# The order of eight heads in a decoder layer's attention: four differential, then four sparse

## The chip, the cores and the metric

The kernel runs on one core of a Trainium2 chip. The metric is the device time of one execution in microseconds (us); the median of several runs is compared.

## What is computed

One decoder layer over 528 tokens (512 and 16 meta tokens) of width 1024: half of a SwiGLU FFN, an attention with two groups of heads side by side, an output projection, and half of a second FFN. The reference, cut to the attention (its two functions compute the queries in blocks of 128):

```python
# differential group, 4 heads, two score maps each (m = 0, 1)
s = einsum('bqhmd,bkhmd->bhmqk', q, k) * A_SCALE + bias
p = softmax(where(k_pos <= q_pos, s, -inf))
a = p[:, :, 0] - lam * p[:, :, 1]
o_a = rmsnorm(einsum('bhqk,bkhd->bqhd', a, v), subln_g) * (1 - lam_init)

# sparse group, 4 heads, one score map each, over the 128 keys
# that an indexer's scores select for every query
_, sel = top_k(score, topk)
s = einsum('bqhc,bqkc->bhqk', q_lat, c[sel]) * B_SCALE + bias
o_b = einsum('bqhc,hcd->bqhd', einsum('bhqk,bqkc->bqhc', softmax(s), c[sel]), w_uv)

h = h + concat([o_a, o_b]) @ w_out
```

All values are 32-bit floats.

## The kernel before

Everything is one program written with a library that records instructions and orders them engine by engine. A matrix product is split into three, of a high and a low part of each operand (hi by hi, hi by lo, lo by hi), so that each product appears as three matmuls. High parts are made by ScalarE (ACT), low parts by VectorE (DVE), as a difference.

The attention works through a list `units` (line 907): for each head in a written-out order, its four blocks of 128 queries (t = 0 to 3, with 144, 272, 400 and 528 keys). `n` is 32 units. A pair (0, hd) in the list is a differential head, (1, hd) a sparse one. The list is the line that the change touches:

```python
    for kind, hd in ((0, 0), (0, 1), (0, 2), (1, 0), (0, 3), (1, 1), (1, 2), (1, 3)):
        units += [(kind, hd, t) for t in range(NQ)]
```

A loop over `i` (from line 1211) pipelines the units. In one pass, unit i has its scores reduced and exponentiated (`u_soft`, lines 999 and 1005), unit i - 1 is normalized (`u_norm`), unit i - 2 is transposed and split (`u_trans`, `u_high`, `u_low`), and the scores of unit i + 1 are computed (`u_scores`).

- `u_scores`: a differential unit has two maps with 64 rows of contraction (line 980), a sparse one a single map with two times 128 rows (line 986). Both are six matmuls per unit, twelve for the 528 keys, which take two pieces of 264. The results go to three PSUM banks, tag "s", used in turn.
- `u_soft`: DVE adds the bias and takes the minimum on the way out of PSUM (line 999, one instruction and a tiny read per map and piece), ACT exponentiates (line 1005).
- `u_norm`: DVE scales and subtracts two maps for a differential unit (lines 1017, 1018), scales one for a sparse unit (line 1020).
- `u_trans`, `u_high`, `u_low`: TensorE (PE) transposes the weights (lines 1027, 1029), ACT makes the high parts, DVE the low parts (lines 1044, 1045). The fourth block is followed by a small cast on DVE (line 1231).
- `u_mask`: for a sparse unit GpSimd (POOL) adds the bias and the selection mask into one of two buffers (line 965).

When a head's fourth block is split, a chain of small steps is started for it and advanced twice per pass. `head_a` multiplies by the values (13 matmuls, line 1054) and normalizes (lines 1064 to 1095). `head_b` multiplies by the latent values twice (26 matmuls), then by `w_uv` (line 1111).

Two more kinds of work lie in the same passes. The latent queries of the sparse heads, `q_latent(hd)`, are made in four chains: 12 matmuls (line 1126), a root mean square, a scaling on DVE (line 1139, four instructions), eight transposes on PE (line 1144) and their splits (lines 1146, 1147). The chain of head hd is started by

```python
        for hd in range(A_H):
            if i == max(QS + 2 * hd, units.index((0, hd, NQ - 1))):
                qchains.append(q_latent(hd))
```

with QS = 7, that is at i = 7, 9, 11 and 19, since the chain of head 3 waits for the fourth block of differential head 3. And once the differential heads 0 to 2 are finished, the output projection is begun for these three heads ahead of time, one eighth (`wo_step`, lines 1162 to 1180) at most of the passes.

The selection of the 128 keys is made by DVE in 16 rounds per block (`topk_round`, lines 759 and 760, and line 763 at the end). These rounds are recorded with a lower priority, so that the library puts them between other work; the last ones, of the fourth block, stand among the units of the fourth head in the list. The bias of the next head is fetched by a DMA on POOL's queue when the scores of the third block are computed (`load_bias`).

Of the kernel before, what the change touches and what calls it, by code (L numbers as in the profile page):

```python
# [200 lines left out]
def layer(ctx: ExitStack, tc: tile.TileContext, xT, gcols, kvg, lamv, rel, onehot,  # L201
# [703 lines left out]

    uku, uvu, buf = [], [], {}
    units = []
    for kind, hd in ((0, 0), (0, 1), (0, 2), (1, 0), (0, 3), (1, 1), (1, 2), (1, 3)):
        units += [(kind, hd, t) for t in range(NQ)]
    n = len(units)  # L910
    st = {}
# [299 lines left out]
    while i < n or chains or qchains or st:  # L1211
# [16 lines left out]
        if 0 <= i - 2 < n and units[i - 2][2] == NQ - 1:  # L1228
            kind, hd, t = units[i - 2]
# [134 lines left out]
```

## Time and profile before

| | |
|---|---|
| median of 3 runs | 1070.76 us (1066.65 to 1071.95) |
| the profiled execution | 1067.94 us, span 1066.2 us |
| PE busy | 1039.1 us, 97% of the span |
| DVE busy | 756.2 us, 71% |
| ACT busy | 522.4 us, 49% |
| mean granted TensorE clock | 0.986 |
| the attention's units | about 483 to 690 us |

The span is the time from the first to the last instruction. The granted clock is TensorE's clock as a share of its full speed: 1.00 is 2.4 GHz, 0.50 is 1.2 GHz. In rows with several engines, "busy (x)" is the time in which the engine had an instruction, and their number. Matmuls overlap their neighbours, so that a matmul's own duration is longer than the step from one start to the next.

### The profile page before, as it was taken

What the parts mean: (1) busy time and instruction counts of PE and PEld (TensorE: products, weight loads), DVE (VectorE), ACT (ScalarE), POOL (GpSimd) and SP (SyncE); (2) the same over time, 40 slices, a digit from 0 to 9 for tenths busy, and PEclk for the clock granted to TensorE, in tenths of its full rate; (3) what the DMA queues carried; (4) which work ended last, traced back from release to release, by engine and by line L of the source; (5) the groups of instructions that cost most, each with busy time, mean ns of one, the idle gap of its engine ahead of it and who ended that gap; (6) DMA issues with size and microseconds to landing.
All of it is one profiled execution on the core that took longest, in us unless ns stands there. A gap on an engine that the chain in (4) does not pass through costs nothing.

```text
span 1066.2 us, 18282 instructions
## 1 busy us (share of the span) xinstructions
PE 1039.1 (97%) x7185; PEld 955.2 (90%) x7185; DVE 756.2 (71%) x1485; ACT 522.4 (49%) x1057; POOL 49.5 (5%) x57
## 2 busy tenths in 40 slices
PE   7999999999999999998999899999999999999998
PEld 7999999999999997997887688788889999988886
DVE  7968999985232246898999878667979999852231
ACT  6626666654222254564546565355546666631111
POOL 0000000000010110000000111030000000000000
PEclk9999999999999999998999789999999999999999
DMA  6263323234333332120220015453333333343331
GB/s 241 80 223 110 101 98 118 87 122 129 104 114 99 116 106 84 60 71 21 90 70 29 20 29 160 144 185 101 117 121 118 103 100 119 129 136 105 116 114 35
DMA packets 38403, 112.58 MB, mean 106 GB/s; under 512 B 4866, under 2 KB 6146, under 8 KB 38316
## 3 DMA queue, kind: packets, MB, share of 16 engines
q1 hardware_dynamic: 36236, 105.64, 30.6%
q0 software_dynamic: 1792, 5.48, 1.5%
q8 instruction: 56, 0.92, 0.3%
q10 hardware_dynamic: 288, 0.29, 0.1%
q14 instruction: 31, 0.25, 0.1%
HBM read 102.98 MB, written 11.44 MB: 107 GB/s over the span
## 4 chain that ended last, share of the span: by engine, by line
PE 87%; DVE 8%; ACT 2%; issue 1%; DMA 1%; ACTq 0%; DVEq 0%
PE d L432 24%; PE X L193 16%; PE V L193 8%; PE g L432 6%; PE u L432 5%; PE nat L708 4%; PE Y L193 4%; PE wo L1162 3%; PE p_ch L925 2%; PE p_ch L664 2%; PE p_ch L1054 2%; PE iq L664 2%; PE p_ch L1162 2%; PE p_s L980 1%; PE p_s L986 1%
## 5 line engine op out<-in xcount | busy, mean ns | idle before, releaser
L101 DVE TENSOR_TENSOR wl<-wr,wh 128x1024 fp32r<-128x1024 f32 (+4 forms) x106 | 120.8, 1142 | 158.8 <-ACT wh L100 157.7
L100 ACT ACTIVATE wh<-wr 128x1024 fp32r<-128x1024 f32 (+4 forms) x106 | 105.4, 995 | 249.1 <-PE d L432 149.2
L432 PE MATMUL d<-AR,wh 128*128 128x264 f32 (+1 forms) x928 | 184.6, 311 | 0.0
L432 PEld LDWEIGHTS d<-AR,wh 128*128 128x128 f32 x928 | 139.5, 188 | 9.8
L193 PE MATMUL X<-AR,ws 128*128 128x256 f32 (+1 forms) x912 | 117.5, 280 | 0.2
L432 PE MATMUL d<-AR,wl 128*128 128x264 f32 (+1 forms) x464 | 115.5, 310 | 0.0
L193 PEld LDWEIGHTS X<-AR,ws 128*128 128x128 f32 x912 | 111.0, 188 | 1.0 <-ACT FA L498 0.8
L174 ACT ACTIVATE ws<-h 128x512 fp32r<-128x512 f32 x140 | 87.7, 628 | 45.4 <-PE X L193 20.4
L175 DVE TENSOR_TENSOR ws<-h,ws 128x512 fp32r<-128x512 f32 x140 | 95.9, 687 | 13.4 <-ACT ws L174 12.2
L432 PEld LDWEIGHTS d<-AR,wl 128*128 128x128 f32 x464 | 75.6, 188 | 4.9
L708 PE MATMUL nat<-wh,hg 128*128 128x256 f32 (+1 forms) x304 | 57.6, 284 | 0.0
L708 PEld LDWEIGHTS nat<-wh,hg 128*128 128x128 f32 x304 | 47.8, 188 | 0.1
L925 PE MATMUL p_ch<-wh,hg 128*128 128x256 f32 x224 | 44.1, 295 | 0.3 <-DVE AR L878 0.3
L708 PE MATMUL nat<-wl,hg 128*128 128x256 f32 (+1 forms) x152 | 43.1, 283 | 0.0
L193 PE MATMUL X<-hg,ws 128*128 128x264 f32 x312 | 42.4, 285 | 0.0
L193 PE MATMUL V<-hg,ws 128*128 128x264 f32 x312 | 42.3, 285 | 0.0
L582 DVE SCALAR_TENSOR_TENSOR h<-d,h 128x528 f32<-128x528 f32 (+1 forms) x16 | 11.2, 700 | 41.1 <-PE d L432 41.1
L432 PE MATMUL d<-hg,wh 128*128 128x512 f32 x128 | 40.0, 393 | 0.0
L193 PEld LDWEIGHTS X<-hg,ws 128*128 128x128 f32 x312 | 39.9, 188 | 0.0
L193 PEld LDWEIGHTS V<-hg,ws 128*128 128x128 f32 x312 | 39.8, 188 | 0.0
L193 PE MATMUL V<-AR,ws 128*128 128x256 f32 x312 | 39.6, 276 | 0.0
L1005 ACT ACTIVATE FA<-FA,mn 128x144 f32<-128x144 f32 (+3 forms) x48 | 27.3, 570 | 25.0 <-DVE mn L999 24.8
(311 smaller groups left out, 2277.9 us busy)
## 6 DMA issues: line engine op xcount, KB each, us to landing
wr<-w1u SPq DMA_DIRECT2D x17, 512.0 KB, 3.6
wr<-w2u SPq DMA_DIRECT2D x17, 512.0 KB, 3.5
wr<-w1d SPq DMA_DIRECT2D x16, 512.0 KB, 3.4
wr<-w2d SPq DMA_DIRECT2D x16, 512.0 KB, 3.5
wr<-w2g SPq DMA_DIRECT2D x15, 512.0 KB, 3.5
wr<-w1g SPq DMA_DIRECT2D x14, 512.0 KB, 3.5
wr<-win_n SPq DMA_DIRECT2D x12, 512.0 KB, 3.4
wr<-win_t SPq DMA_DIRECT2D x9, 512.0 KB, 3.4
```

The source lines that it names most:

```text
L100: self.nc.scalar.activation(hi[:, c], r[:, c], AF.Copy)
L101: (low or self.low).tensor_sub(lo[:, c], r[:, c], f32(hi[:, c]))
L174: self.nc.scalar.activation(hi, x, AF.Copy)
L175: V.tensor_sub(lo, x, f32(hi))
L193: self.nc.tensor.matmul(ps, l[:, w], self.rhs(q, r, k), start=(p in FIRST and k == 0 and x == 0), stop=(k == KC // 2 - 1 and x == 2), skip ...
L432: PE.matmul(ps[:, i, : b - a], w[:, k, :], x(kk)[:, a:b], start=(kk == 0 and p_ == 0), stop=(kk == ktot - 1 and p_ == 2))
L664: PE.matmul(o, w[:, k, :], x[:, k, a:b], start=(k == 0 and p_ == 0), stop=(k == KC - 1 and p_ == 2))
L708: PE.matmul(ps, xx[:, kk, a:b], w[:, k, :], start=(kk == 0 and p_ == 0), stop=(kk == KC - 1 and p_ == 2))
L925: PE.matmul(ps, xx[:, kk, a:b], w[:, kk % 4, :], start=(kk == 0 and p_ == 0), stop=(kk == KC - 1 and p_ == 2))
L1005: A.activation(s, s, AF.Exp, scale=-1.0, bias=mn, accum_out=sums[:, m: m + 1])
L1054: PE.matmul(oo, l, r, start=(x == 0), stop=(x == len(seq) - 1))
L1162: PE.matmul(ps, w[:, k, :], x[k0 + k], start=(k == 0 and p_ == 0), stop=(k == nk - 1 and p_ == 2))
```

## The change

The list of heads is written in another order. Nothing else is edited.

```diff
-    for kind, hd in ((0, 0), (0, 1), (0, 2), (1, 0), (0, 3), (1, 1), (1, 2), (1, 3)):
+    for kind, hd in ((0, 0), (0, 1), (0, 2), (0, 3), (1, 0), (1, 1), (1, 2), (1, 3)):
         units += [(kind, hd, t) for t in range(NQ)]
```

The head at place p uses buffer `bsel[p]` for its weights and bias table p % 2, so differential head 3 and sparse head 0 change buffers with their places. The chain `q_latent(3)` now starts at i = 15. `q_latent(0)` to `q_latent(2)` and the passes of the output projection stay where they were.

The instructions are the same; what moves is their order. On PE, before, from the last scores of sparse head 0 to the transposes of the latent query of head 2 (p_s are the score banks, p_tr and p_ch other banks, FA holds scores and weights, buf_ql the latent query):

```order
L986 MATMUL p_s<-AR 128x264 x5
L1069 MATMUL p_ch<-onesr,buf_vv 128x1 x4
L980 MATMUL p_s<-AR 128x144 x3
L1027 MATMUL p_ch<-ident,FA 128x128 x2
L1029 MATMUL p_ch<-ident,FA 16x128
L1144 MATMUL p_ch<-ident,buf_ql 128x128 x4
L1027 MATMUL p_tr<-ident,FA 128x128 x3
L1029 MATMUL p_tr<-ident,FA 16x128
L980 MATMUL p_s<-AR 128x144 x3
```

The same place with the change, between the chain of differential head 2 and the transposes of the latent query of head 2:

```order
L1069 MATMUL p_ch<-onesr,buf_vv 128x1 x4
L980 MATMUL p_s<-AR 128x264 x3
L1027 MATMUL p_ch<-ident,FA 128x128 x2
L1029 MATMUL p_ch<-ident,FA 16x128
L980 MATMUL p_s<-AR 128x264 x6
L1027 MATMUL p_tr<-ident,FA 128x128 x3
L1029 MATMUL p_tr<-ident,FA 16x128
L986 MATMUL p_s<-AR 128x144 x6
L986 MATMUL p_s<-AR 128x272 x6
L986 MATMUL p_s<-AR 128x400 x4
L1078 MATMUL p_ch<-ident,ray 4x128
L1144 MATMUL p_ch<-ident,buf_ql 128x128 x4
```

The scores of differential head 3 (line 980) have come ahead, and 16 score matmuls of sparse head 0 (line 986) stand in one piece ahead of the transposes of line 1144.

On DVE, before, from the last round of the selection to the scaling of that latent query (line 1139):

```order
L760 MATCH_REPLACE FA<-m_5415,FA 128x528
L307 SCALAR_TENSOR_TENSOR rqw<-rqw,rqy 128x4
L1045 TENSOR_TENSOR hg<-p_tr,hg 16x128
L763 TENSOR_SCALAR FA<-FA 128x528
L308 SCALAR_TENSOR_TENSOR rqy<-rqw,rqy 128x4
L1014 RECIPROCAL rs<-sums 128x1
L1095 TENSOR_TENSOR AR<-R,AR 128x512
L1139 TENSOR_SCALAR buf_ql<-buf_ql,rqy 128x256 x4
```

With the change, from the same round on:

```order
L760 MATCH_REPLACE FA<-m_5415,FA 128x528
L999 ISA FA,mn<-p_s,FA 128x400
L999 ISA mn 128x1
L763 TENSOR_SCALAR FA<-FA 128x528
L1044 TENSOR_TENSOR hg<-p_tr,hg 128x128
L1045 TENSOR_TENSOR hg<-p_tr,hg 16x128
L1014 RECIPROCAL rs<-sums 128x2
L1095 TENSOR_TENSOR AR<-R,AR 128x512
L1017 TENSOR_SCALAR FA<-FA,rs,lam 128x400
L999 ISA FA,mn<-p_s,FA 128x264
L999 ISA mn 128x1
L1018 SCALAR_TENSOR_TENSOR FA<-FA,rs 128x400
```

The scaling of line 1139 now follows 13 rows after the last of these, behind the other reductions of differential head 3's fourth block; the reduction of 400 keys and the first one of 264 keys are those that free the two banks which the last scores of that block need.

## Rows read from the trace of the kernel before

**Rows 1.** The page: PE's busy time, and the granted clock in 40 slices.
```profile
PE 1039.1 (97%) x7185; PEld 955.2 (90%) x7185; DVE 756.2 (71%) x1485; ACT 522.4 (49%) x1057; POOL 49.5 (5%) x57
...
PEclk9999999999999999998999789999999999999999
```

**Rows 2.** Windows: stretch, its length, busy time of each engine, clock, DMA share, GB/s.
```profile
580.00:600.00 20.00, 17.30 (x117) 13.95 (x113) 18.87 (x65) 14.83 (x49) 2.40 (x3) 1.00 0.05 14
600.00:620.00 20.00, 18.11 (x62) 12.96 (x63) 13.89 (x44) 8.94 (x27) 3.15 (x4) 0.50 0.05 15
```

**Rows 3.** Windows of the attention (PE, PEld, DVE, ACT, POOL, then the clock).
```profile
486.00:488.00 2.00, 0.07 (x1) 0.07 (x1) 1.97 (x8) 0.03 (x1) 0.00 (x0) 0.88 0.00 0
...
598.00:600.00 2.00, 0.18 (x2) 0.00 (x0) 1.94 (x7) 0.53 (x2) 0.34 (x1) 1.00 0.00 0
600.00:602.00 2.00, 0.39 (x2) 0.32 (x2) 2.00 (x5) 0.00 (x0) 1.70 (x2) 0.54 0.00 0
...
618.00:620.00 2.00, 2.00 (x8) 1.81 (x8) 0.69 (x1) 1.54 (x5) 0.00 (x0) 0.50 0.00 0
620.00:622.00 2.00, 2.00 (x12) 1.84 (x11) 0.62 (x2) 1.50 (x5) 0.00 (x0) 0.84 0.00 0
...
601.60:620.60 19.00, 18.71 (x64) 13.56 (x65) 12.29 (x42) 9.54 (x29) 1.75 (x3) 0.50 0.05 16
586.30:602.30 16.00, 11.97 (x77) 10.11 (x77) 14.99 (x45) 9.45 (x35) 3.79 (x3) 0.93 0.06 17
```

**Rows 4.** What PE waited for, 440 to 690 us (total, times, longest).
```profile
PE p_ch L1144 <- DVE buf_ql L1139: 3.4, 1, 3.4
PE p_s L980 <- DVE mn L999: 3.0, 1, 3.0
```

**Rows 5.** Order of time on PE (start, length, line, shape, count, idle before).
```profile
592.99 1.78 PE L1054 MATMUL p_ch<-h,AR 128*128 128x512 f32 x11
...
601.61 1.27 PE L1144 MATMUL p_ch<-ident,buf_ql 128*128 128x128 f32 x4 [3.42 <-DVE buf_ql L1139]
...
618.43 5.25 PE L1054 MATMUL p_ch<-hg,AR 128*128 128x512 f32 x25
623.62 0.87 PE L980 MATMUL p_s<-AR 64*128 64x264 f32 x8
...
638.20 0.28 PE L1126 MATMUL p_ch<-wh,AR 128*128 128x256 f32 x1
638.32 0.28 PE L1126 MATMUL p_ch<-wl,AR 128*128 128x256 f32 x1
...
659.17 1.63 PE L986 MATMUL p_s<-AR 128*128 128x264 f32 x12
```

**Rows 6.** Order of time on DVE, 586 to 628 us.
```profile
586.18 0.16 DVE L308 SCALAR_TENSOR_TENSOR ray<-raw,ray 128x4 f32<-128x4 f32 x1
...
600.16 2.18 DVE L1139 TENSOR_SCALAR buf_ql<-buf_ql,rqy 128x256 f32<-128x256 f32 x4
...
604.37 0.41 DVE L1044 TENSOR_TENSOR hg<-p_ch,hg 128x256 fp32r<-128x256 f32 x1
...
612.10 0.42 DVE L1231 CAST hg<-hg 16x512 fp32r<-16x512 f32 x1
...
627.80 1.14 DVE L1139 TENSOR_SCALAR buf_ql<-buf_ql,rqy 128x256 f32<-128x256 f32 x4
```

**Rows 7.** DVE's busy time, one line each: 999 (two stretches), 1017, 1018, 1020.
```profile
587.50:605.30 17.80, 2.24 (x10) 0.86 0.05 16
605.40:626.80 21.40, 4.32 (x20) 0.64 0.04 10
...
609.00:624.60 15.60, 1.25 (x3) 0.63 0.05 13
...
609.00:624.60 15.60, 1.50 (x3) 0.63 0.05 13
...
587.50:605.30 17.80, 1.05 (x3) 0.86 0.05 16
```

## The prediction

> **What bounds the kernel now.** I read the page first, then the kernel in stretches of 20 us, then the attention in stretches of 2 us, then what TensorE (PE) waited for there, and last the order of time on PE and VectorE (DVE). The page says that PE is busy for 97% of the span and that the chain of work is PE's [rows 1]; a stretch in which PE stands still, or runs at half clock, is therefore paid in full. The profile's clock line has three slices below 9 (8, 7 and 8), all in the attention [rows 1]. By 20 us, DVE is the fuller engine up to 600 us (18.87 of 20 us, PE 17.30), and from 600 to 620 us PE runs at a granted 0.50, 1.2 instead of 2.4 GHz [rows 2].
>
> The reader is to see three things in the finer views. First, PE stood still before both falls of the clock: 3.0 us for DVE's score reduction and 3.4 us for DVE's scaling of the latent query of head 2 [rows 4]. In the first case the clock's mean in 486 to 488 is 0.88, so it fell while PE did next to nothing (0.07 us) [rows 3]; in the second PE was busy for 0.18 and 0.39 us of two 2 us stretches, and the clock went from 1.00 to 0.54 in the second of them [rows 3]. Second, the half clock stayed although PE was then busy almost without a break: 18.71 of 19.00 us [rows 3]. It rose in the stretch 620 to 622, after PE had gone over to the 25 value matmuls that start at 618.43 [rows 3, 5]. At half clock half of the busy time is lost, 18.7 / 2 = 9.4 us. Third, DVE sets the pace before the fall: from 586.3 to 602.3 it is busy 14.99 of 16.00 us [rows 3].
>
> **What the change moves.** No instruction is added or removed. Differential head 3 goes from the fifth place to the fourth, sparse head 0 from the fourth to the fifth. The order is the same up to the square-root refinement that DVE ends at 586.34 (start 586.18, 0.16 long) [rows 6], and again from the scores of sparse head 3 on; all terms lie between. A differential unit costs DVE more: head 3's ten score reductions take 4.32 us, head 0's five 2.24; normalizing its first three blocks takes 1.25 + 1.50 us, where three blocks of the sparse head take 1.05 [rows 7].
>
> *DVE up to the latent query of head 2.* Before, 16.0 us, to 602.34 [rows 6]. Now all of head 3's reductions stand in this piece, 4.32 us, where three of head 0's five stood (2.24 less 0.42, 0.49 and 0.05: 1.3 us); and its normalizing, 2.75 us, where two blocks of the sparse head stood (two thirds of 1.05: 0.7 us). One more split of weights comes in (0.41) [rows 6], and three tiny instructions beside it, for which I take as much again. That is 3.0 + 2.05 + 0.8 = 5.9 us more. Two things go: the scaling took 2.18 us while GpSimd was busy for 1.70 of 2 us, and 1.14 elsewhere [rows 3, 6], and those additions of GpSimd come later now (1.0 us); and DVE's own wait in the piece, at most 16.00 - 14.99 = 1.0 us, of which I take 0.5. So the piece takes 16.0 + 5.9 - 1.5 = 20.4 us and ends at 606.7.
>
> *DVE up to the end of head 3's weights.* 18 instructions, from the refinement to the cast, of forms that occur before from 602.3 to 612.5 [first and last, rows 6]. There 31 of them took 10.2 us; 18/31 of it is 5.9, and I take 6.3, since the large forms are among them. DVE is through at 613.0.
>
> *PE.* While DVE works off these 26.7 us, PE gets its scores and transposes one by one, and it cannot end head 3's value matmuls before DVE's last split. Eleven of them take 1.78 us [rows 5], so PE has them at about 614.5. At that point it has done, from 582.4 on, what it had done before at 623.62, except nine latent-query matmuls (0.12 each by start to start [rows 5]; 1.05 us) and 13 value matmuls (11 in 1.78, so 2.3 with two more), but eleven score matmuls of head 3 more (8 in 0.87 [rows 5]; 1.2). So before is 2.2 us of work ahead there. After it PE is the fuller engine in both orders. The gain with the clock at full is 623.6 - 614.5 - 2.2 = 6.9 us. I take 6.2, for waits of DVE that the order does not show; with 0.5 to 2 us of such waits it is 4.5 to 7.
>
> *The queues that are passed.* GpSimd fetches the bias of the next head at the third block of the head before it; head 3's bias now takes that place, and head 0's follows. Each is asked for two blocks and more ahead of its use, and costs nothing behind DVE's work; if it were late, DVE would wait at the head's first reduction. SP's loads for the output projection keep their units and lie beside PE. ScalarE's exponentials move with their units; both maps of head 3's third block are done when DVE asks for their sums, or a few tenths of a us later (within the 2 us above).
>
> *The clock.* This is the term that the trace does not show. Of the 9.4 us the gain above counts all as saved. But a new hole opens for PE: between about 598 and 603 us it has one group of 128-wide transposes and six of head 3's score matmuls, some 0.9 us of work, because the last scores wait for the bank that DVE's first reduction of the fourth block frees. The longest standstill in it: between the two reductions that free its last two banks DVE has six other instructions (the order in the section on the change), about 2.4 us by their forms with the second reduction; PE fills 0.3 of that, and 2.1 us are left. The bounds: nothing, if the clock holds; and, if it falls, all PE work from there to the end of head 3's values at half clock. That is 16 sparse scores (12 of the 264 wide take 1.63 us [rows 5], so some 2.3 in all), the transposes, small products and other scores behind them (5.9 us by their places in the order) and the 13 values (2.3): 10.5 us, doubled, less the 1.8 us in which PE would have stood: 8.7 us. In between lies a fall that ends with the 16 sparse scores, which come in one piece, as the 25 values did: 2.3 us. I take the fall with the early rise, as before both falls came in such poor stretches and both rises in unbroken ones.
>
> **What page and trace say of it.** The rows: both falls followed a standstill of 3.0 and 3.4 us [rows 4]. The Trainium skill, in "TensorE: Matmul & The Clock Gate", section "HAM oscillation — how this bites in real kernels", has it that a long idle gap between bursts of matmuls brings the half clock, and that one avoids it by keeping such gaps out. By that rule the new standstill, shorter than either, would leave the clock alone and the sum be -6.2 us instead of -3.9. The trace agrees as to the gaps, but the clock had fallen in 600 to 602, before the gap of rows 4 ended, and after a stretch of small work; so I don't rest on it.
>
> **The sum.** -6.2 + 2.3 = -3.9 us on the profiled execution's 1067.94 us: 1064.0. The median of the three runs is 1070.76, 2.8 us above that execution, which lies within their 1066.65 to 1071.95; taken off the median it is **1066.9 us**, -0.4%.
>
> **Rivals**, each against the median.
> 1. *The clock holds in the new hole* (the rule above as a mechanism of this kernel). For it: the longest standstill is a third shorter than those of rows 4. Against: 0.9 us of work in 5 us. -6.2 us: 1064.6.
> 2. *The clock falls and stays down until the values of head 3*: slower than before. It decides where the 16 sparse scores are not enough to bring it back, as the mixed work from 602 to 618 was not [rows 3]. -6.2 + 8.7 = +2.5 us: 1073.3.
> 3. *PE and DVE go on waiting for each other in the sparse heads*, since three score banks bind each unit to the one before. PE stood 20 - 17.30 = 2.7 us in 580 to 600 [rows 2]; as much in each of the three stretches up to 674 is +8.1, in all +4.2 us: 1075.0. Against: a sparse unit gives DVE half of the reductions and PE twice as many value matmuls [rows 7].
> That the change does nothing is excluded: the order of PE and DVE differs from 582 us to the scores of sparse head 3.
>
> **How the numbers follow.** Forecast 0.42, rival 1 0.25, rival 2 0.22, rival 3 0.11. A change under 0.5% (5.35 us) can't be told from none here: the three runs alone differ by 5.3 us. Faster by more (under 1065.4): 0.6 of rival 1 and 0.4 of the forecast, 0.32. Slower by more (over 1076.1): 0.15 of rival 2, a little under half of rival 3 and a share for a fall that lasts longer than its bound, 0.10. Within: 0.58. The range, 1061 to 1074.5, reaches from rival 1 with its gain of 7 us and a run on the fast side to rival 2 with a us to spare, and leaves out most of rival 3. The likeliest case's own range is 1063 to 1070.
>
> **What would show it.** Right: the wait of 3.4 us for the scaling is gone; DVE is over 90% busy from 586 to about 613; PE has its poor stretch near 598 to 603 with a longest wait of about 2 us, for a score reduction, and a shorter piece at 0.50 than 20 us behind it; the same work ends 2 to 6 us sooner from 670 on, and everything behind it moves by as much. Wrong: a clock of 1.00 throughout (rival 1), 0.50 up to 615 or more (rival 2), or PE standing over 2 us in a stretch of 20 between 615 and 675 (rival 3). If the second piece of DVE took over 8 us, or a bias came late, the sum itself would be wrong.

## The result, and the profile after

The changed kernel takes 1075.79 us (median of 13 runs, 1071.3 to 1080.31) against 1067.88 us (13 runs, 1066.07 to 1071.95) before: a ratio of 1.0073, 95% interval 1.006 to 1.0086. It is **slower by 7.9 us**, and above the predicted range. The profiled execution took 1075.79 us with a span of 1074.0 us, 7.8 us more than the span before, so its trace holds the whole difference.

The page of the changed kernel, PE's busy time and the granted clock in 40 slices, against [rows 1]:

```profile
PE 1045.2 (97%) x7185; PEld 963.1 (90%) x7185; DVE 758.4 (71%) x1485; ACT 522.4 (49%) x1057; POOL 48.5 (5%) x57
...
PEclk9999999999999999998998689999999999999999
```

PE is busy 6.1 us longer with the same 7185 matmuls. Where three slices in a row read 9, 7 and 8 before, they read 8, 6 and 8 now. From 582 us on, up to a place near the end of the attention, one window of the kernel before (length, busy PE, PEld, DVE, ACT, POOL, then the clock):

```profile
582.00:700.00 118.00, 110.86 (x607) 90.58 (x608) 90.47 (x261) 65.61 (x190) 17.25 (x18) 0.91 0.28 88
```

The same window of the changed kernel, up to the same place, 7.8 us later:

```profile
582.00:707.80 125.80, 116.09 (x609) 97.14 (x608) 93.10 (x261) 65.43 (x191) 17.50 (x20) 0.85 0.26 83
```

Before, PE stood still for 118.00 - 110.86 = 7.1 us, now for 125.80 - 116.09 = 9.7 us. So 2.6 us of the 7.8 are more standing still, and 5.2 us are the same work done at a lower clock (0.85 instead of 0.91). Counted another way, length times clock is 118.00 x 0.91 = 107.4 us before and 125.80 x 0.85 = 106.9 us now: the lower clock alone is enough for the whole difference. Windows of the changed kernel show where the clock is low (2 us each, and one of 20):

```profile
582.00:584.00 2.00, 1.42 (x10) 1.00 (x9) 1.94 (x9) 1.76 (x6) 0.00 (x0) 0.83 0.00 0
584.00:586.00 2.00, 2.00 (x12) 1.58 (x13) 2.00 (x10) 1.02 (x3) 0.54 (x1) 0.50 0.00 0
582.00:602.00 20.00, 19.30 (x71) 13.94 (x70) 17.66 (x58) 11.18 (x36) 2.08 (x3) 0.53 0.05 14
602.00:604.00 2.00, 2.00 (x9) 1.78 (x8) 0.82 (x3) 1.08 (x6) 0.00 (x0) 0.55 0.00 0
604.00:606.00 2.00, 1.31 (x10) 1.18 (x10) 0.00 (x0) 1.79 (x5) 0.00 (x0) 1.00 0.00 0
606.00:608.00 2.00, 1.57 (x9) 0.90 (x8) 0.00 (x0) 1.43 (x6) 0.00 (x0) 0.80 0.02 4
614.00:616.00 2.00, 2.00 (x15) 1.74 (x15) 2.00 (x5) 0.85 (x4) 1.28 (x1) 0.99 0.01 4
630.00:632.00 2.00, 1.86 (x11) 1.64 (x12) 1.81 (x9) 1.39 (x6) 0.62 (x2) 0.78 0.26 55
```

The clock fell at about 583.3 us (windows of 0.25 us read 1.00 up to 583.25 and 0.50 from 583.50), some 17 us sooner than before [rows 3], and was at 0.50 up to 603.8; it fell again within 606 to 608 and within 630 to 632. The order of time on PE around the first fall, and where the clock came back:

```profile
579.90 0.65 PE L980 MATMUL p_s<-AR 64*128 64x264 f32 x6
580.69 1.05 PE L1069 MATMUL p_ch<-onesr,buf_vv 128*128 128x1 f32 x8
581.61 0.42 PE L1027 MATMUL p_ch<-ident,FA 128*128 128x128 f32 x2
581.86 0.27 PE L1029 MATMUL p_ch<-ident,FA 128*16 128x128 f32 x1
582.06 0.63 PE L980 MATMUL p_s<-AR 64*128 64x264 f32 x3
582.62 0.66 PE L1144 MATMUL p_ch<-ident,buf_ql 128*128 128x128 f32 x4
583.87 0.87 PE L1027 MATMUL p_tr<-ident,FA 128*128 128x128 f32 x3 [0.58 <-DVE FA L1018]
584.53 0.42 PE L1029 MATMUL p_tr<-ident,FA 128*16 128x128 f32 x1
584.88 1.69 PE L980 MATMUL p_s<-AR 64*128 64x144 f32 x9
...
600.57 3.19 PE L1054 MATMUL p_ch<-h,AR 128*128 128x512 f32 x11
```

From 579.9 on there are 64-row scores, one-column products and transposes. The wait of 0.58 us begins as the clock falls; from 570 us up to there no wait was over 0.2 us. Up to the first four transposes of line 1144 this is also the work of the kernel before, which did it at a clock of 1.00. What differs is what follows. Where the nine scores of line 980 stand at 584.88, the kernel before has scores of sparse head 0, with 128 rows:

```profile
582.42 1.09 PE L1144 MATMUL p_ch<-ident,buf_ql 128*128 128x128 f32 x8
...
584.18 2.09 PE L986 MATMUL p_s<-AR 128*128 128x144 f32 x11
```

What PE of the changed kernel waited for, 560 to 700 us (total, times, longest), against [rows 4]:

```profile
PE p_ch L1054 <- DVE hg L1044: 3.2, 2, 2.7
PE p_s L980 <- DVE mn L999: 2.1, 1, 2.1
PE p_ch L1078 <- DVE ray L308: 2.0, 1, 2.0
```

The wait of 3.4 us for the scaling of line 1139 is gone; three others have come or grown (that for line 1044 was 1.4 us in all before). On DVE the two points that the prediction had timed are late, behind a wait of 4.79 us for exponentials (line 1005). On ScalarE these stand behind a copy (line 1064) that waited for the eleven value matmuls of line 1054, which PE did at half clock. The copy on ScalarE, then DVE (start, length, line):

```profile
604.16 0.60 ACT L1064 ACTIVATE buf_vv<-p_ch 128x512 f32<-128x512 f32 x1 [1.04 <-PE p_ch L1054]
...
608.11 0.17 DVE L1014 RECIPROCAL rs<-sums 128x2 f32<-128x2 f32 x1 [4.79 <-ACT FA L1005]
...
612.42 1.14 DVE L1139 TENSOR_SCALAR buf_ql<-buf_ql,rqy 128x256 f32<-128x256 f32 x4
...
620.98 0.42 DVE L1231 CAST hg<-hg 16x512 fp32r<-16x512 f32 x1
```

### The profile page after: what moved, and what is told of

Its sections match the earlier page's. It is cut to its first block, busy times and chain, and to the rows that moved or that the text cites. A ratio compares the mean times of both kernels' runs of the same rounds, so it can differ in the third digit from the quotient of the medians.

```text
span 1074.0 us, 18277 instructions
## 1 busy us (share of the span) xinstructions
PE 1045.2 (97%) x7185; PEld 963.1 (90%) x7185; DVE 758.4 (71%) x1485; ACT 522.4 (49%) x1057; POOL 48.5 (5%) x57
## 4 chain that ended last, share of the span: by engine, by line
PE 89%; DVE 6%; ACT 2%; issue 1%; DMA 1%; ACTq 0%; DVEq 0%
PE d L432 23%; PE X L193 16%; PE V L193 8%; PE g L432 6%; PE u L432 5%; PE nat L708 4%; PE Y L193 4%; PE p_ch L925 3%; PE wo L1162 3%; PE p_ch L1054 2%; PE p_ch L664 2%; PE iq L664 2%; PE p_s L986 2%; PE p_ch L1162 2%; PE p_s L980 1%
## 5 line engine op out<-in xcount | busy, mean ns | idle before, releaser
L432 PE MATMUL g<-AR,wh 128*128 128x264 f32 x192 | 34.3, 300 | 6.4 <-ACT AR L324 6.4
```

Of the source, the lines that this page charges most:

```text
L432: PE.matmul(ps[:, i, : b - a], w[:, k, :], x(kk)[:, a:b], start=(kk == 0 and p_ == 0), stop=(kk == ktot - 1 and p_ == 2))
```

## The experiments

Theory T1: the change lost by the clock. With four differential heads in a row PE has, from 580 us on, a mix of work at which the granted clock goes to half, whether PE stands still or not. Rival R1: the loss is that PE, DVE and ACT wait for each other in that order. A second rival is that any standing still makes the clock fall. The edit used in most runs adds matmuls to the loop over the units, whose result nobody reads, in the passes of a list:

```diff
+    def keep_busy(i):
+        if i not in PASSES:
+            return
+        kb = bank("ch")
+        for _ in range(K):
+            PE.matmul(kb[:, :512], vah[:, 1, 0:P], vah[:, 2, :512], start=True, stop=True)
...
             u_soft(i)
+        keep_busy(i)
         advance(qchains, 1)
...
             score_step(i + 1)
+        keep_busy(i)
```

**1 and 2: both orders with 128-row matmuls added.** Changed order: `PASSES = 11..17`, K = 2.

> The changed order, with two matmuls of 128x512 whose result nobody reads put in twice per pass of the loop over the units, in passes 11 to 17 (28 in all; by the step of the value matmuls at full clock, 1.78 us for eleven of mixed width, they add some 6 us where PE is not waiting). Theory T1 (the changed order lost by the clock: it falls at 582.7 us and stays at 0.50 for most of 582 to 640): the clock is at or near 1.00 in 582 to 640, and although PE has 6 us more to do the time is 4 us or more under the changed kernel's 1075.8. Theory R1 (four differential heads in a row make PE, VectorE and ScalarE wait for each other, whatever the clock): the clock may hold, but the time is 1075 to 1082, as PE only has more to do.

Order before: `PASSES = 11..19`, K = 2.

> The order before, with the same matmuls in passes 11 to 19 (36, some 7.7 us of PE time). T1: the fall at 600 us goes too, which gives back up to 9.4 us and costs up to 7.7: 1063 to 1069. With the clock held in both orders the difference between this kernel and the changed order with the same matmuls is under 3 us, where it was 8 without them. R1: the difference stays at 6 to 10 us.

Measured: 1075.32 us (1068.91 to 1078.78, ten runs) for the changed order, 1068.03 (1062.72 to 1069.82) for the order before. The median of the first lies in R1's range, that of the second in T1's. The added matmuls began at 581.47 us, and in the profiled run of the first kernel the clock fell near 583 all the same and was at half for most of the time up to 603. Its ten runs lie in two groups: four of 1068.91 to 1070.16 us with a mean clock of 0.991 to 0.994, six of 1075.26 and more with 0.986 or 0.987. The same kernel so has a long stretch of half clock in some executions and not in others. The second kernel's run with the highest clock (0.998) is its fastest, 1062.72. So time went with the clock, but the difference of the two medians, 7.3 us, stayed as R1 had it. Inconclusive: the added work came too late to hold the clock in most runs.

**3: the same with 4 rows.** In the first kernel:

```diff
-            PE.matmul(kb[:, :512], vah[:, 1, 0:P], vah[:, 2, :512], start=True, stop=True)
+            PE.matmul(kb[:, :512], vah[:4, 1, 0:P], vah[:4, 2, :512], start=True, stop=True)
```

> As the first kernel, but the added matmuls contract over 4 rows instead of 128: the same number and the same 512 columns, so PE is busy as long. If it is PE's standing still that makes the clock fall, it holds here as with 128 rows and the two kernels agree within 2 us. If it is the kind of work (T1: only 64-row scores, transposes and small products stood there), the clock falls as in the changed kernel, and 28 more matmuls at 0.2 to 0.4 us make it 1080 or more. R1 (waits alone): as the first kernel, within 2 us.

Measured: 1089.4 us, mean clock 0.972 to 0.976. The second outcome: 14 us above the 128-row version.

**4: one part undone, the start of the latent query of head 3.**

```diff
-            if i == max(QS + 2 * hd, units.index((0, hd, NQ - 1))):
+            if i == max((QS, QS + 2, QS + 4, 19)[hd], units.index((0, hd, NQ - 1))):
```

> The changed order, but the chain of the latent query of head 3 starts at pass 19, as before the change, instead of 15. T1: the 12 wide matmuls that open this chain came at 592.7 us and did not bring the clock back, so without them the first fall is as it was; later they may shorten the fall at 630 us. Within 3 us of 1075.8. R1: the chain's squares and scaling leave the stretch in which VectorE and ScalarE are full, and the time is 2 to 5 us lower.

Measured: 1075.06 us, as the changed kernel. Where this chain starts is no part of the loss. In its trace the first fall came at 581.0 us, in work that is still that of the order before.

**5: the order before, 12 matmuls at its fall.** `PASSES = 14..16`, K = 2.

> The order before, with the unread 128x512 matmuls in passes 14 to 16 only, around the fall at 600 us: 12 of them, some 2.6 us of PE time, of which a part lies in PE's own waits there. T1 (the clock is what counts): the fall at 600 us goes, and with it up to 9.4 us of half clock; 1059 to 1064. If the clock there matters little: 1067 to 1070.

Measured: 1063.37 us, ratio 0.9952 (0.994 to 0.9964), in T1's range. More work and less time: the half clock after 600 us was paid for on the path that sets the end. It was not all removed; half clock from about 606 to 613 us is left in its trace.

**6 and 8: the changed order, ahead of its first fall, with 128 rows and with 4.** `PASSES = 10..12`, K = 4; run 8 with the 4-row form of run 3.

> The changed order, with the same matmuls in passes 10 to 12 only, four at a time, twice per pass (24, some 5.1 us): they stand ahead of the fall at 582.7 us, where those of the first experiment began at 581.5. T1: the first fall goes, or comes after 592 us; that fall cost some 10 us of PE time, so the time is 3 us or more under the changed kernel's (1073 or less). R1 (waits alone): the added work is added time, 1078 to 1082.

> The changed order with the 24 added matmuls of the sixth run at the same places (passes 10 to 12) and of the same 512 columns, but contracting over 4 rows instead of 128. T1 in the form that the kind of work decides: the clock falls near 582 as in the changed kernel and the added work is done at half clock: 1080 to 1090. If it is only that PE is kept busy, the result is that of the sixth run, 1066 to 1071.

Measured: **1068.85 us** with 128 rows (12 runs, 1064.64 to 1070.8), **1080.74 us** with 4 (1080.3 to 1080.81). Windows of run 6:

```profile
580.00:584.00 4.00, 4.00 (x25) 3.35 (x26) 3.94 (x15) 2.02 (x8) 0.00 (x0) 1.00 0.00 0
584.00:588.00 4.00, 3.06 (x24) 2.22 (x22) 2.78 (x16) 2.73 (x6) 0.54 (x1) 1.00 0.14 17
592.00:596.00 4.00, 4.00 (x28) 3.08 (x26) 4.00 (x12) 3.19 (x12) 0.00 (x0) 1.00 0.00 0
```

The same windows of run 8:

```profile
580.00:584.00 4.00, 4.00 (x22) 2.81 (x19) 3.94 (x15) 1.23 (x6) 0.00 (x0) 0.69 0.00 0
584.00:588.00 4.00, 4.00 (x12) 2.39 (x13) 0.12 (x2) 0.66 (x3) 0.00 (x0) 0.50 0.00 0
592.00:596.00 4.00, 4.00 (x14) 2.31 (x12) 3.01 (x11) 1.62 (x8) 1.21 (x2) 0.50 0.26 70
```

This pair decides for T1 at the first fall. The same 24 matmuls of 512 columns stand at the same places; with 128 rows the clock is 1.00 up to 600 us though PE pauses for almost 1 us in 584 to 588, with 4 rows it falls at 581.5 although PE is busy for 4.00 of 4.00 us. Against the changed kernel the added work costs 5.0 us where it doesn't hold the clock (1080.74 - 1075.79); where it does, the kernel is 6.9 us faster in spite of it (1075.79 - 1068.85).

**7: a third order.**

```diff
-    for kind, hd in ((0, 0), (0, 1), (0, 2), (0, 3), (1, 0), (1, 1), (1, 2), (1, 3)):
+    for kind, hd in ((0, 0), (0, 1), (0, 2), (1, 0), (1, 1), (0, 3), (1, 2), (1, 3)):
```

> A third order: differential heads 0, 1, 2, then sparse 0 and 1, differential 3, sparse 2 and 3. T1: the value matmuls of two sparse heads and the first eighths of the output projection, all 128 rows, stand beside the scores of differential head 3, so less PE time passes at half clock than before (under 15 us between 580 and 700): 1058 to 1066. R1: the chain of the latent query of head 3 starts only at pass 23 and PE waits for it ahead of sparse head 3: 1068 to 1075.

Measured: **1060.6 us** (1059.97 to 1061.23), ratio 0.993 (0.9918 to 0.9942): faster than both kernels by its order alone. Windows of the kernel before:

```profile
596.00:600.00 4.00, 2.11 (x15) 1.63 (x14) 3.94 (x16) 2.21 (x8) 0.34 (x1) 1.00 0.00 0
600.00:604.00 4.00, 2.39 (x10) 1.51 (x10) 3.93 (x12) 0.74 (x2) 1.95 (x2) 0.52 0.22 68
604.00:608.00 4.00, 3.72 (x19) 3.10 (x19) 3.60 (x14) 3.09 (x10) 1.20 (x2) 0.50 0.03 6
608.00:612.00 4.00, 4.00 (x14) 2.66 (x13) 3.28 (x11) 0.74 (x2) 0.00 (x0) 0.50 0.00 0
```

The same windows of this order:

```profile
596.00:600.00 4.00, 0.79 (x6) 0.44 (x5) 3.94 (x13) 1.26 (x6) 1.36 (x1) 0.79 0.00 0
600.00:604.00 4.00, 3.35 (x15) 3.15 (x16) 3.44 (x13) 1.56 (x3) 1.75 (x3) 0.50 0.26 72
604.00:608.00 4.00, 3.85 (x26) 3.56 (x26) 3.87 (x11) 3.24 (x13) 1.05 (x1) 0.86 0.01 2
608.00:612.00 4.00, 4.00 (x27) 3.40 (x26) 3.35 (x12) 3.55 (x14) 1.76 (x2) 1.00 0.17 49
```

Both fall in the same wait for the scaling of line 1139. What stands behind it differs: here, in PE's order of time,

```profile
600.65 1.97 PE L1144 MATMUL p_ch<-ident,buf_ql 128*128 128x128 f32 x8 [3.84 <-DVE buf_ql L1139]
...
603.18 2.28 PE L986 MATMUL p_s<-AR 128*128 128x144 f32 x9
```

sparse scores, and the clock is back within 604 to 608; before, 64-row scores stand there, and it is back within 620 to 622 [rows 3].

**9 and 10: DVE relieved, in both orders** (12 of the 16 selection rounds of the last block are left out).

```diff
-                    for r in range(TOPK // 8):
+                    for r in range(TOPK // 8 if t < NQ - 1 else 4):
                         topk_round(t)
```

> The changed order with 4 of 16 selection rounds for the last block of 128 queries; 12 rounds (some 1.5 us of VectorE each) are left out, so the sparse heads see other keys in that block. VectorE is then far less full up to 598 us, PE's work is the same. T1: the clock still falls between 580 and 590, as the work there is still 64-row scores, transposes and small products, and the kernel stays 5 us or more above the order before with the same rounds left out. R1 (VectorE's lateness makes the loss): the fall goes or comes after 595, and the two orders end within 3 us of each other.

> The order before with the same 12 selection rounds left out. PE's wait of 3.4 us for the scaling at 601.6 goes, as VectorE is through sooner. If the standstill made the fall at 600 us, it goes too: 1056 to 1061. If the kind of work makes it (64-row scores, transposes and small products from 597 us on), it stays in part: 1061 to 1066.

Measured: 1072.51 us (1069.11 to 1073.9) and 1059.13 us (1057.33 to 1060.88). The changed order with the short selection, windows:

```profile
580.00:584.00 4.00, 4.00 (x24) 3.30 (x24) 3.65 (x15) 1.78 (x8) 0.00 (x1) 0.80 0.00 0
584.00:588.00 4.00, 3.20 (x16) 2.17 (x14) 3.33 (x13) 3.45 (x11) 1.32 (x2) 0.50 0.27 68
...
592.00:596.00 4.00, 4.00 (x13) 2.81 (x12) 1.39 (x3) 2.02 (x7) 0.00 (x0) 0.50 0.00 0
```

DVE is down to 1.39 of 4 us and PE is still at half clock; ahead of the fall PE waited for 0.2 us at most. Taking DVE's load away widened the gap of the two orders from 7.9 to 13.4 us, where R1 wanted it under 3. In the order before, the time came out in the range that was set for a fall made by the standstill (1056 to 1061), but the trace speaks against that outcome: the wait of 3.4 us went, and yet some 10 us of half clock (about 602 to 612) stayed, with no wait over 0.5 us close ahead of it. That fall does not need the standstill either. The same trace has a short fall, from about 588.5 to 591.9 us:

```profile
588.00:592.00 4.00, 4.00 (x17) 3.41 (x18) 3.17 (x9) 3.05 (x12) 1.96 (x3) 0.57 0.14 40
```

Ahead of it, from 583 us on, stand sparse scores and 128-row products of line 1126 along with small work, and no wait that the profile lists. So 64-row scores are not the whole condition, and which mix makes the clock fall is not settled by these runs.

**11: the third order with 12 matmuls at its fall.** `PASSES = 13..15`, K = 2.

> The order of the seventh run (sparse 0 and 1 ahead of differential 3) with the unread 128x512 matmuls in passes 13 to 15 (12, some 2.6 us, of which up to 3 lie in PE's wait of 3.84 us at 600 us). T1: the fall at 597 us, which cost that run some 4 us of PE time, goes, and the time is 1056 to 1060. If that clock loss is hidden behind VectorE there: 1060 to 1063.

Measured: 1060.91 us, no gain over run 7, in the second range. A fall is left near 602 and another shows near 581, so the clock was not held, and the run tells nothing on what the fall costs. The one near 581 tells something else:

```profile
580.00:584.00 4.00, 4.00 (x21) 3.41 (x21) 3.69 (x14) 2.52 (x8) 0.45 (x1) 0.61 0.00 0
584.00:588.00 4.00, 3.90 (x29) 3.45 (x28) 3.91 (x14) 3.97 (x14) 0.74 (x2) 0.96 0.24 68
```

Up to there this kernel gives PE the work of the kernel before, so that the fall at this place is not the changed order's alone. Here it lasted from 580.9 to 584.3, with sparse scores following at 583.52; in the changed kernel, without them, 20 us. By these two traces the change took away what ended the fall, and not only what kept it from coming.

**12: the changed order, at all three places.** `PASSES = 10, 11, 12, 19, 20, 25`, K = 4.

> The sixth run (the changed order with the unread 128x512 matmuls, four at a time, twice per pass, in passes 10 to 12) with the same in passes 19, 20 and 25 too, around PE's two later waits of 2.0 us (for the refinement of line 308) and 2.7 us (for the weights' low parts of line 1044), each followed by half clock for some 8 us in the sixth run. 24 matmuls more, 5.1 us, of which up to 4.7 can lie in the waits. If the later falls are paid in full: they go, up to 8 us come back, and the time is 1061 to 1066. If VectorE sets the pace there and hides them: 1068 to 1073.

Measured: 1069.19 us (1067.59 to 1074.59), as run 6. The clock is 1.00 around both later waits now (in run 6 it was down to 0.50 behind them), yet the time didn't move: what the clock gave back, the 5 us of added work took. Whether those two falls cost anything by themselves stays open; the fall of run 6 near 604 us is longer here (0.62 and 0.52 in 604 to 612).

## Why the prediction was wrong

**DVE's pace: right, where PE kept the clock.** The prediction had the scaling of line 1139 end at 606.7 us and head 3's value matmuls at about 614.5. In run 6, with the clock at 1.00 up to 603 us and a fall of some 3 us behind that, the two points read 606.5 and 615.4, and DVE was busy for 26.07 of the 27.00 us from 586 to 613:

```profile
605.36 1.14 DVE L1139 TENSOR_SCALAR buf_ql<-buf_ql,rqy 128x256 f32<-128x256 f32 x4
```

```profile
613.20 2.20 PE L1054 MATMUL p_ch<-hg,AR 128*128 128x512 f32 x12
```

In the changed kernel the first stands at 613.6 and the cast at 620.98, 8 us behind the 613.0 forecast. DVE there stood 4.79 us behind line 1005, and so behind PE's value matmuls at half clock (eleven took 3.19 us, 1.92 in run 6). In run 6 its longest wait in this piece was 1.2 us. So DVE no longer set the pace.

**The step that failed: the clock's term.** It began at a new hole near 598 us, with the clock at full up to there, and its bounds, 0 to 8.7 us, counted only work behind that hole. The clock had already been at half for 20.5 us before it, and no term and no rival had that fall. PE was busy for 19.82 us of it; at half clock half of that is lost, an estimate of 9.9 us, where the sum had nothing. The later fall at 631 us, 7.0 us of work and so 3.5 us by the same estimate, was not in it either. The gain of 6.2 us counted the 9.4 us of half clock before as saved; instead a stretch as long came back 17 us earlier.

The hole itself fits, in part by luck. The 16 sparse scores behind it did bring the clock back, as taken, and PE was busy for 4.70 us of that fall (607.2 to 614.0), half of which is the 2.3 us of the sum. But the wait of 2.10 us, forecast as 2.1, has another cause than the one given: DVE's reduction was late because DVE itself stood still until 608.11. In run 6, where it did not, PE's longest wait for a score reduction is 0.3 us.

The prediction looked for the fall in a stretch where PE has little to do. Run 9 (a fall with no wait over 0.2 us ahead) and the pair of 4 and 128 rows show that here the kind of work counts, and it had read this in its own rows (18.71 of 19.00 us busy at 0.50 [rows 3]) and used it only for how long a fall lasts, not for where one starts.

**The rule of the skill.** Ahead of the fall at 583.3 us, from 570 us on, no wait was over 0.2 us, and in run 9 none either. The Trainium skill, in "TensorE: Matmul & The Clock Gate", section "HAM oscillation — how this bites in real kernels", puts the half clock down to long idle gaps; the trace does not agree, and the measurement decides. Rival 1, which rested on that rule, is out.

**Rivals 2 and 3.** Rival 2 had the right sign and, of the first fall, the right kind of loss, at the wrong place: 1073.3. Rival 3 (1075.0) is there in part: two waits of 2.0 and 2.7 us in the sparse heads (the waits above), and 2.6 us more standing still in all, where it had 8.1. Its number is the nearest, and that is luck. The pair of runs 6 and 8 shows that holding the first fall is worth 7 us with the work added for it; the pair itself differs by 11.9 us, part of which is the added work at half clock.

What the changed order costs with the clock at full in both was not measured: in the runs that come near it (0.995 and 0.996), it stands at 1067.59 to 1069.19 with some 10 us of added work (run 12), the order before at 1064.58 and 1065.74 with some 8 us (run 2). The times and clocks of all runs allow an estimate. Time multiplied by the mean granted clock of the same run has a median of 1053.5 us over the 13 runs of the changed kernel and of 1053.1 us over the 64 runs of the kernel before that were timed with the experiments; run 4 gives 1053.3, the third order 1054.5. By this the orders need nearly the same time at full clock, and the 7.9 us are the clock's. The waits that came are then no price on top of it.

## What to carry to other kernels

Before moving work, read for each stretch of the busiest engine not only where it waits but what it does: here a stretch of mostly 64-row scores, small products and transposes ran at half clock for 20 us, busy nearly all the time. Ask of every reordering which 128-row matmuls stood between the small ones and would end a fall, and price the clock wherever that mix changes, not only at new holes. Where a wait can't be avoided, try 128-row matmuls behind it: the order that had them there (run 7) is 0.7% faster than before. And time such a kernel more than once: with the same work the clock fell in some executions and not in others (run 1).

## What the hardware showed that was not expected

The granted clock fell with PE busy for 4.00 of 4.00 us (run 8), and held in a stretch with a pause of 0.94 us (run 6); 24 matmuls that differ only in 4 or 128 rows of contraction made 11.9 us of difference. The Trainium skill, in "TensorE: Matmul & The Clock Gate", section "Part 1: The HAM clock gate", says that the gate follows how busy PE has been. Busy time as the profile counts it was higher in run 8, which had the lower clock: there PE was busy without a break from 576.0 us up to the fall at 581.5. And a DVE instruction of 128x4 (line 308), 0.15 to 0.32 us in the kernel before, took 1.28 us where PE waited 2.0 us for it. An addition of GpSimd (line 965) ran from 628.77 to 630.06 us, nearly the same time; that the one made the other was not tried:

```profile
628.80 1.28 DVE L308 SCALAR_TENSOR_TENSOR ray<-raw,ray 128x4 f32<-128x4 f32 x1
```
